# Splits and sums of the output projection's operands, written in another order in a two-layer decoder kernel

## The chip, the cores and the metric

The kernel runs on one core of a Trainium2 chip. The core has five instruction streams that work side by side and meet at semaphores: TensorE (PE, matrix products and transposes; its weight loads are listed as PEld), VectorE (DVE), ScalarE (ACT), GpSimd (POOL) and SyncE (SP), whose stream here only issues transfers between HBM and on-chip memory. The metric is the device time of one execution in microseconds (us), lower is better; the time of a kernel is the median of its runs.

## The reference, cut to what matters

```python
def stick_breaking_attention(q, k, v):           # per 128-query block i
    z = einsum('bqhd,bkhd->bhqk', q_blk, k_blk) * DH ** -0.5
    log_1m = where(mask, log_sigmoid(-z), 0.0)    # mask: key strictly before query
    rev = cumsum(log_1m, axis=3, reverse=True)
    w = where(mask, exp(log_sigmoid(z) + (rev - log_1m)), 0.0)
    out = einsum('bhqk,bkhd->bqhd', w, v_blk)

# layer 1 (layer 0 has gated linear attention in its place)
q = h @ sb_w_q;  o = stick_breaking_attention(q, k_shared, v_shared)
h = layer_norm(DEEPNORM_ALPHA * h + o @ sb_w_o, ln_g[1, 0], ln_b[1, 0])
h = layer_norm(DEEPNORM_ALPHA * h + relu(h @ mlp_w_up[1]) ** 2 @ mlp_w_down[1], ln_g[1, 1], ln_b[1, 1])
```

The sequence has 512 rows, the model 1024 columns, the attention 16 heads of 64, the MLP 4096 columns. All is float32.

## The kernel before, in words

**Arithmetic.** A float32 operand is split into two rounded parts, hi (made by ScalarE, a copy with a narrower type) and lo (the rest, made by VectorE as operand minus hi). A product is then three matmuls: hi by hi, lo by hi, hi by lo (`mm3`, L93 to L95). Splits of weights are `split_tile` (L70 on ScalarE, L72 on VectorE, or on GpSimd where `pool` is handed in); splits of activations are `put` (L98, L99). A weight piece is 128x1024: its raw form arrives by a transfer on SP's queue into one of three buffers (`raw`), its parts go to six buffers each (`hi`, `lo`).

**Stages.** Layer 0 (gated linear attention, LayerNorm, MLP), the shared K and V projection, then layer 1: attention by eight pairs of heads, output projection, LayerNorm, MLP, LayerNorm.

**Attention.** The loop over `p` (L1071) handles one pair in each pass. `weights()` of a pair takes the scores (L943 on PE, into six PSUM banks), adds the mask (L960, VectorE), two sigmoids (L964, L965, ScalarE) and a scan that runs along the keys (L968, VectorE; the listing of instructions calls it SCALAR_TENSOR_TENSOR). `turn()` of the pair in the next pass transposes the five blocks of weights (L977 on PE, four 128x128 transposes each) and moves them out of PSUM into two `wt` tiles, one for each head (L982 on ScalarE). These moves are called evictions below. `outputs()` (L991 on PE) multiplies them with V into one bank, `ops`. Between the transposes PE works on filler: the projection of a later pair's K or Q, for the last pair the first products of the output projection. The query projection's result is split by L931 (ScalarE) and L932 (VectorE).

**Output projection.** It is done with seven products of half size in place of eight, so its operands are sums and differences of the attention output's halves. `o1` holds the output of pairs 0 to 3, `o2` that of pairs 4 to 7; a11 and a21 are the two column halves of `o1`, a12 and a22 those of `o2`. For pairs 4 to 7, `sums` replaces a slice of a21 by a22 minus itself (L1068) and a slice of a11 by its negative plus the difference `less` (both 128x256 on VectorE, L1049 is the second). The names first to seventh stand for the seven operands: `seventh` is the split of `less` (128x1024), `sixth` and `fifth` are the splits of a11 and a21, `third` that of a12 minus a11 (L1049 again, this time 128x1024, `minus(a12, a12, a11)`). Their products are the PE matmuls of L1039. `LATER` (L1147) is the product of a12 or a22 columns themselves (`whole`), whose lo part for the first two slices is made by L1100 of the kernel before. Weights go with them as b1 to b7; b2 comes through `raw` with its lo on GpSimd. `project()` yields after each of four row tiles, and `finish` then does that tile's LayerNorm: `bn_stats` (L177) and `bn_aggr` (L182) on VectorE, reciprocal root on GpSimd (L183, L184), centring on VectorE (L190), eight transposes on PE (L231), scale and shift on ScalarE (L234) and the split of the result (L98, L99), which is the operand of the MLP's first matmuls. The four residual row tiles are `h`; L167 and L169 add product results to them.

**MLP.** `up` (L706) takes its first weights from the list `up0`, four pieces made inside `project()` (L1168, L1172, L1177). Its first half works on row tiles 0 and 1, the second on 2 and 3.

**What sets the order.** A scheduler puts each engine's instructions in an order by readiness and program position; each engine then executes its own list strictly in order and waits where an operand or a buffer is not ready. Instructions wrapped in `keep` (`tc.keep_in_program_order`) hold their written order among themselves. SP's queue of transfers is a list too.

Of the kernel before, what the change touches and what calls it, by code (L numbers as in the profile page):

```python
# [9 lines left out]
F32R = mybir.dt.float32r  # L10
I32 = mybir.dt.int32
AF = mybir.ActivationFunctionType
# [22 lines left out]
def yoco_kernel(ctx: ExitStack, tc: tile.TileContext, x, gla_w_in, gla_w_a2, gla_b_a, gla_norm_g,  # L35
                gla_w_o, kv_w, sb_w_q, sb_w_o, mlp_w_up, mlp_w_down, ln_g, ln_b, out):
    nc = tc.nc
# [20 lines left out]
    def unit(dtype):  # L58
        return big.tile([P, 4, 512], dtype, tag="T", bufs=8, name=nm("T"))
# [19 lines left out]
    def pieces_512(w, r0, nkt, c0, **how):  # L79

        got = []
        for kp in range(nkt // 2):
            hi, lo = split_piece(block(w, r0 + 256 * kp, c0), 2, **how)
            got += [(hi[:, 0, :], lo[:, 0, :]), (hi[:, 1, :], lo[:, 1, :])]
        return got
# [11 lines left out]
    def put(hi, lo, ps, keep=lambda ins: ins, on=None):  # L97
        keep(nc.scalar.activation(hi, ps, AF.Copy))  # L98
        keep((on or nc.vector).tensor_tensor(lo, ps, hi.bitcast(F32), op=ALU.subtract))  # L99
# [909 lines left out]
    def fetch(bs, k, j, onto=False):  # L1009
        for h, b in enumerate(bs):  # L1010
            to = b.rearrange("p (a b) -> p a b", a=2)
            if onto:
                tc.keep_in_program_order(nc.gpsimd.dma_start(out=to, in_=w_o(k, h, j), accum_op=ALU.add))
            else:
                tc.keep_in_program_order(nc.sync.dma_start(out=to, in_=w_o(k, h, j)))
# [48 lines left out]
    ys, us, xs = ([None, None] for _ in range(3))  # L1064
    full = slice(0, 4)

    def sums(k, o):
        tt(a21[:, k, :], o[:, HI], a21[:, k, :], op=ALU.subtract)  # L1068
        minus(a11[:, k, :], o[:, HI], less[:, k, :])

    for p in range(NP):  # L1071
        made = pairs[p].turn()
        take = lambda at: lambda n: [next(made, None) for _ in range(at.get(n, 0))]
        if p + 2 < NP:
            pairs[p + 1].queries()
            if p == 0:
                subtract(keep)
            elif p < NT:
                hs[p].affine(vec, keep)
            pairs[p + 2].keys(take(TAKE))  # L1080
        elif p + 1 < NP:
            pairs[p + 1].queries(take(FILL))
        else:
            mid = take(FILLS)

            def then(n):
                mid(n)
                if n == 11:
                    keep(nc.scalar.activation(o2h[:, 0:2, :], o2[:, 0:2, :], AF.Copy))

            run(STEPS, halves(first), b1, ys, closes=False, mid=mid)
            run(STEPS[:4], halves(seventh), b7, us, closes=False, mid=lambda n: then(8 + n))
        for _ in made:
            pass
        if p < NP - 2:
            pairs[p + 1].weights()
            if p == 1:
                differences(1)()
        if p == NP - 1:
            tt(o2l[:, 0:2, :], o2[:, 0:2, :], o2h[:, 0:2, :].bitcast(F32), op=ALU.subtract)  # L1100
            put(o2h[:, 2, :], o2l[:, 2, :], o2[:, 2, :], keep)
            sums(2, o2[:, 2, :])
            for s in range(2):
                add(s, ys, 0, 0)
        ops = pairs[p].outputs(ALL if p < NP - 2 else LAST)
        if p < 4:
            nc.scalar.activation(o1[:, p, :], ops, AF.Copy)
        else:
            if p == 4:
                o2 = unit(F32)  # L1110
                a12, a22 = o2[:, :, LO], o2[:, :, HI]
            if p == NP - 1:
                put(o2h[:, 3, :], o2l[:, 3, :], ops)
            if p != NP - 2:
                sums(p - 4, ops)
            nc.scalar.activation(o2[:, p - 4, :], ops, AF.Copy)
        if p == 3:
            first = unit(F32R)
            into(first, a11, full)
            less = sbp.tile([P, 4, 256], F32, name="less")  # L1120
            tt(less, a11, a21, op=ALU.subtract)
        if p == NP - 3:
            b1 = pieces_512(sb_w_o[0], 0, 4, 0)
            b22 = wide()
            fetch(b22, 1, 1)
            fetch(b22, 0, 1, True)
        if p == NP - 2:
            b7 = pieces(b22)
            fetch(b22, 0, 0, True)
            b5 = [both(tag).bitcast(F32).rearrange("p a b -> p (a b)") for tag in ("k", "q")]  # L1130
            fetch(b5, 0, 0)
            fetch(b5, 0, 1, True)
            b2 = pieces_512(sb_w_o[0], 512, 4, 0, **pool)
            pairs[p + 1].weights()
            seventh, o2h, o2l = unit(F32R), unit(F32R), unit(F32R)
            into(seventh, less, full)

    b6 = pieces(b22)
    sixth, fifth = unit(F32R), unit(F32R)
    into(sixth, a11, full)  # L1140
    into(fifth, a21, full)
    h3T = Split()
    whole = lambda c0: lambda k, s: tuple(o[:, k, c0 + P * s:c0 + P * s + P] for o in (o2h, o2l))

    def project():
# [6 lines left out]
        run(STEPS, halves(sixth), b6, ys, False, False)  # L1152
        for s in range(2):
            add(s, ys, 1, 0)
        minus(a12, a12, a11)
        third = unit(F32R)
        into(third, a12, full)
        add(0, us, 1, 1)
# [15 lines left out]
        add(0, us, 1, 0, last=True)  # L1174
        yield 2
        yield ~1
        up0.extend(pieces_512(mlp_w_up[1], 512, 4, 0))  # L1177
        run(STEPS[4:], whole(256), b4, us, False)
        add(1, us, 1, 0, last=True)
        yield 3  # L1180
# [79 lines left out]
```

## Time and profile before

| | before |
|---|---|
| median of 3 runs | 1114.59 us (1114.31 to 1114.91) |
| the profiled execution, its own time | 1115.89 us |
| its span, first to last instruction | 1114.2 us |
| mean granted TensorE clock | 0.997 |
| PE busy | 1102.6 us, 99% of the span |
| VectorE busy | 818.2 us, 73% |
| ScalarE busy | 572.1 us, 51% |
| GpSimd busy | 145.4 us, 13% |
| chain that ended last | 90% on PE |

The profiled execution is 1.30 us longer than the median of the runs. In rows of the timeline the first number is the start in us from the span's start, the second the length, then engine, line, operation, output and inputs, shapes, and xN for N instructions merged; in square brackets stands how long the engine had been idle before and what ended it. A matmul's length contains its pipeline, so the next one starts before it has ended. Windows give, for a stretch of time, the busy time of each engine with the count of instructions, then the granted TensorE clock as a share of full speed.

### The profile page before, as it was taken

Reading aid. Unit: us, or ns where it says so; the run is one execution under the profiler, and the core shown is the slowest. Engines: PE = TensorE matmul, PEld = TensorE weight load, DVE = VectorE, ACT = ScalarE, POOL = GpSimd, SP = SyncE. Lnnn points to the kernel's source line nnn. Section 1 sums busy time; section 2 is a strip of 40 time slices with the busy share of each in tenths; the row PEclk is TensorE's granted clock in tenths of the full one; section 3 lists DMA queues with packets and bytes.
Section 4 is the critical chain, followed back from the end, with each engine's and each line's share of the span. In section 5 each row is a group of like instructions: output and inputs, shape, how many; then the busy total and the mean of one; then the engine's idle time right before and its main releaser. Section 6 shows DMA issues by size and latency. Waiting matters only on the chain.

```text
span 1114.2 us, 14380 instructions
## 1 busy us (share of the span) xinstructions
PE 1102.6 (99%) x5503; PEld 913.9 (82%) x5503; DVE 818.2 (73%) x1029; ACT 572.1 (51%) x853; POOL 145.4 (13%) x177
## 2 busy tenths in 40 slices
PE   9999999999999999999999999999999999999997
PEld 7888888898888888888888777788988888888885
DVE  4677639957966856858899886688489767667677
ACT  4455437653533534536675667666545435336363
POOL 1011223200100100122302200211100000001222
PEclk9999999999999999999999999999999999999999
DMA  7441399492670670788746353443937816706774
GB/s 241 130 133 57 115 251 204 138 301 90 188 208 20 201 208 25 196 202 151 225 100 184 107 134 96 101 76 97 302 109 205 237 34 174 223 20 189 177 128 92
DMA packets 111352, 169.06 MB, mean 152 GB/s; under 512 B 13178, under 2 KB 38138, under 8 KB 111284
## 3 DMA queue, kind: packets, MB, share of 16 engines
q1 hardware_dynamic: 86228, 119.39, 32.7%
q0 software_dynamic: 22592, 44.04, 22.8%
q10 hardware_dynamic: 2464, 4.72, 1.2%
q8 instruction: 43, 0.70, 0.3%
q14 instruction: 25, 0.20, 0.1%
HBM read 162.89 MB, written 3.15 MB: 149 GB/s over the span
## 4 chain that ended last, share of the span: by engine, by line
PE 90%; DMA 5%; DVE 2%; issue 1%; POOL 1%; ACT 1%; SPq 0%; POOLq 0%; DVEq 0%; ACTq 0%
PE ps L355 28%; PE ps L93 16%; PE ps L94 16%; PE ps L95 16%; DMA B<-in_gla_w_o_dram 5%; PE ps L796 3%; PE ps L1039 3%; PE ps L991 2%; PE ps L977 2%; PE ps L943 2%; PE ps L231 1%; DVE bst L177 0%; DMA h<-in_x_dram 0%; POOL B L314 0%; PE ps L584 0%
## 5 line engine op out<-in xcount | busy, mean ns | idle before, releaser
L355 PE MATMUL ps<-hi,T 128*128 128x512 f32 x1008 | 313.3, 390 | 0.1
L93 PE MATMUL ps<-T,hi 128*128 128x512 f32 (+1 forms) x776 | 290.2, 375 | 0.0
L94 PE MATMUL ps<-T,hi 128*128 128x512 f32 (+1 forms) x776 | 287.4, 371 | 1.8 <-DVE T L99 1.7
L95 PE MATMUL ps<-T,lo 128*128 128x512 f32 (+1 forms) x776 | 287.0, 370 | 0.0
L72 DVE TENSOR_TENSOR lo<-raw,hi 128x1024 fp32r<-128x1024 f32 x126 | 153.2, 1222 | 95.9 <-ACT hi L70 95.6
L70 ACT ACTIVATE hi<-raw 128x1024 fp32r<-128x1024 f32 x128 | 135.4, 1061 | 169.5 <-PE ps L94 55.1
L355 PEld LDWEIGHTS ps<-hi,T 128*128 128x128 f32 x1008 | 189.0, 188 | 39.8 <-DVE T L99 0.6
L70 ACT ACTIVATE hi<-B 128x1024 fp32r<-128x1024 f32 x118 | 124.4, 1059 | 175.1 <-PE ps L94 105.4
L72 DVE TENSOR_TENSOR lo<-B,hi 128x1024 fp32r<-128x1024 f32 x118 | 143.1, 1223 | 85.8 <-ACT hi L70 85.8
L355 PE MATMUL ps<-lo,T 128*128 128x512 f32 x504 | 196.2, 389 | 0.0
L94 PEld LDWEIGHTS ps<-T,hi 128*128 128x128 f32 x776 | 146.4, 189 | 25.7 <-DVE T L99 2.3
L95 PEld LDWEIGHTS ps<-T,lo 128*128 128x128 f32 x776 | 146.2, 188 | 24.7
L93 PEld LDWEIGHTS ps<-T,hi 128*128 128x128 f32 x776 | 146.1, 189 | 24.3 <-issue 1.0
L314 POOL DMA_DIRECT2D B<-in_mlp_w_down_dram x52 | 62.9, 1262 | 544.2 <-DMA B<-in_mlp_w_down_dram 357.8
L355 PEld LDWEIGHTS ps<-lo,T 128*128 128x128 f32 x504 | 94.7, 188 | 19.6
L169 DVE TENSOR_TENSOR h<-h,ps 128x512 f32<-128x512 f32 x108 | 73.3, 681 | 2.7 <-PE ps L355 2.4
L99 DVE TENSOR_TENSOR T<-s,T 128x1024 fp32r<-128x1024 f32 (+1 forms) x52 | 54.8, 1056 | 9.6 <-ACT T L98 9.6
L98 ACT ACTIVATE T<-s 128x1024 fp32r<-128x1024 f32 (+1 forms) x52 | 48.4, 935 | 21.2 <-DVE s L721 14.1
L968 DVE TENSOR_TENSOR_SCAN c<-r,c 128x384 f32<-128x384 f32 (+2 forms) x64 | 49.4, 819 | 3.3 <-ACT c L965 3.2
L93 PE MATMUL ps<-hi,T 128*128 128x512 f32 x128 | 51.5, 402 | 0.0
L719 ACT ACTIVATE s<-ps 128x512 f32<-128x512 f32 x64 | 38.0, 594 | 25.9 <-PE ps L95 25.2
L95 PE MATMUL ps<-hi,T 128*128 128x512 f32 x128 | 50.3, 393 | 0.0
(212 smaller groups left out, 1295.4 us busy)
## 6 DMA issues: line engine op xcount, KB each, us to landing
raw<-in_mlp_w_up_dram SPq DMA_DIRECT2D x64, 512.0 KB, 5.2
B<-in_mlp_w_down_dram SPq DMA_DIRECT2D x64, 512.0 KB, 5.5
B<-in_mlp_w_down_dram POOLq DMA_DIRECT2D x52, 512.0 KB, 7.4
raw<-in_gla_w_in_dram SPq DMA_DIRECT2D x20, 512.0 KB, 3.8
raw<-in_mlp_w_down_dram SPq DMA_DIRECT2D x16, 512.0 KB, 4.4
B<-in_gla_w_o_dram POOLq DMA_DIRECT2D x14, 512.0 KB, 9.5
raw<-in_kv_w_dram SPq DMA_DIRECT2D x12, 512.0 KB, 4.8
B<-in_gla_w_o_dram SPq DMA_DIRECT2D x8, 512.0 KB, 6.0
```

The lines of the kernel that those rows point to most:

```text
L70: keep(nc.scalar.activation(hi, raw, AF.Copy))
L72: keep((on or nc.vector).tensor_tensor(lo, raw, hi.bitcast(F32), op=ALU.subtract))
L93: keep(nc.tensor.matmul(ps, lhsT=a[0], rhs=b[0], start=first, stop=False))
L94: keep(nc.tensor.matmul(ps, lhsT=a[0], rhs=b[1], start=False, stop=False))
L95: keep(nc.tensor.matmul(ps, lhsT=a[1], rhs=b[0], start=False, stop=last))
L98: keep(nc.scalar.activation(hi, ps, AF.Copy))
L99: keep((on or nc.vector).tensor_tensor(lo, ps, hi.bitcast(F32), op=ALU.subtract))
L169: nc.vector.tensor_tensor(h, h, ps, op=op)
L314: nc.gpsimd.dma_start(out=b.rearrange("p (a b) -> p a b", a=2), in_=weights(k, h, j), accum_op=ALU.add)
L355: nc.tensor.matmul(banks[s], lhsT=a(k, s)[x], rhs=b[k][y], start=opens and (k, x, y) == (0, 0, 0), stop=closes and (k, x, y) == (3, 1, 0), ...
L719: nc.scalar.activation(s2[:, f, :], pss[f], AF.Relu)
L968: nc.vector.tensor_tensor_scan(down, r[:, at][:, ::-1], down, 0.0, op0=ALU.mult, op1=ALU.add)
```

## The change

Five things are written differently.

- `sums` reads the copy in `o2` in place of the PSUM bank, and the copy (L1116 before) is written ahead of it. `sums` takes an optional `keep`.
- The split of `less` into `seventh` moves from the end of pass 6 to behind the evictions of pass 6, pinned with `keep`.
- `sums(2)`, the slice of pair 6, moves from pass 7 to pass 6, behind the scores and weights of pair 7, pinned; b2's pieces are written behind it.
- `minus(a12, a12, a11)` moves from the middle of `project()` to ahead of it, behind the splits of `sixth` and `fifth`, pinned.
- The last two of the four first up-projection pieces are pinned.

```diff
-    def sums(k, o):
-        tt(a21[:, k, :], o[:, HI], a21[:, k, :], op=ALU.subtract)
-        minus(a11[:, k, :], o[:, HI], less[:, k, :])
+    def sums(k, o, keep=lambda ins: ins):
+        keep(tt(a21[:, k, :], o[:, HI], a21[:, k, :], op=ALU.subtract))
+        keep(minus(a11[:, k, :], o[:, HI], less[:, k, :]))
...
         for _ in made:
             pass
+        if p == NP - 2:
+            seventh, o2h, o2l = unit(F32R), unit(F32R), unit(F32R)
+            put(seventh[:, :, LO], seventh[:, :, HI], less, keep)
         if p < NP - 2:
...
             put(o2h[:, 2, :], o2l[:, 2, :], o2[:, 2, :], keep)
-            sums(2, o2[:, 2, :])
             for s in range(2):
...
                 put(o2h[:, 3, :], o2l[:, 3, :], ops)
+            nc.scalar.activation(o2[:, p - 4, :], ops, AF.Copy)
             if p != NP - 2:
-                sums(p - 4, ops)
-            nc.scalar.activation(o2[:, p - 4, :], ops, AF.Copy)
+                sums(p - 4, o2[:, p - 4, :])
...
+            pairs[p + 1].weights()
+            sums(2, o2[:, 2, :], keep)
             b2 = pieces_512(sb_w_o[0], 512, 4, 0, **pool)
-            pairs[p + 1].weights()
-            seventh, o2h, o2l = unit(F32R), unit(F32R), unit(F32R)
-            into(seventh, less, full)
...
     into(sixth, a11, full)
     into(fifth, a21, full)
+    keep(minus(a12, a12, a11))
...
-        minus(a12, a12, a11)
         third = unit(F32R)
...
-        up0.extend(pieces_512(mlp_w_up[1], 512, 4, 0))
+        up0.extend(pieces_512(mlp_w_up[1], 512, 4, 0, keep=keep))
```

How the instructions move is seen at three places. The first is ScalarE in pass 6, from the copy of pair 5's output to the copy of pair 6's; `T<-less` is the hi part of `seventh`, `hi<-raw` the second piece of b2, `q` the hi part of pair 7's query. Before:

```order
L1116 ACTIVATE T_6074<-ps_6247 128x512
L982 ACTIVATE wt_6293<-ps_6295 128x4x128
L98 ACTIVATE T_6456<-less 128x4x256
L982 ACTIVATE wt_6294<-ps_6304 128x4x128
L982 ACTIVATE wt_6293<-ps_6316 128x3x128
L982 ACTIVATE wt_6293<-ps_6316 128x128
L982 ACTIVATE wt_6294<-ps_6326 128x3x128
L982 ACTIVATE wt_6294<-ps_6326 128x128
L70 ACTIVATE hi_6386<-raw_6384 128x1024
L931 ACTIVATE q_6336<-ps_6283 128x512
L982 ACTIVATE wt_6293<-ps_6339 128x2x128
L982 ACTIVATE wt_6294<-ps_6339 128x2x128
```

and after the change:

```order
L1116 ACTIVATE T_6074<-ps_6247 128x512
L982 ACTIVATE wt_6293<-ps_6295 128x4x128
L982 ACTIVATE wt_6294<-ps_6304 128x4x128
L982 ACTIVATE wt_6293<-ps_6316 128x3x128
L982 ACTIVATE wt_6293<-ps_6316 128x128
L982 ACTIVATE wt_6294<-ps_6326 128x3x128
L982 ACTIVATE wt_6294<-ps_6326 128x128
L70 ACTIVATE hi_6459<-raw_6457 128x1024
L931 ACTIVATE q_6336<-ps_6283 128x512
L982 ACTIVATE wt_6293<-ps_6339 128x2x128
L982 ACTIVATE wt_6294<-ps_6339 128x2x128
L98 ACTIVATE T_6346<-less 128x4x256
```

The split of `less` has gone from the second eviction's place to behind the last one. Pair 5's copy stands at the same place in both lists; before it waits for VectorE and PE, now for PE alone.

The second is VectorE at the end of pair 7's scans and in front of the `LATER` product. After the change, from the last scan on:

```order
L968 SCALAR_TENSOR_TENSOR c_6442<-r_6441,c_6442 128x256 x2
L1068 TENSOR_TENSOR T_5008<-T_6074,T_5008 128x256
L1049 SCALAR_TENSOR_TENSOR T_5008<-T_6074,less 128x256
L167 SCALAR_TENSOR_TENSOR h_1637<-h_1637,ps_6463 128x512
L72 TENSOR_TENSOR lo_6565<-d_6271,hi_6563 128x1024
L167 SCALAR_TENSOR_TENSOR h_1638<-h_1638,ps_6476 128x512
L72 TENSOR_TENSOR lo_6569<-d_6272,hi_6567 128x1024
L167 SCALAR_TENSOR_TENSOR h_1639<-h_1639,ps_6503 128x512
L1103 TENSOR_TENSOR T_6348<-T_6074,T_6347 128x1024
```

The second and third rows are `sums(2)`. Before, they stood in front of pair 7's first mask addition (L960), and the row with `h_1637` followed the last scan directly; the last row is `LATER`'s lo part for its first two slices (L1100 before, L1103 after).

The third is VectorE between the centring of row tile 0 and the split of row tile 1 (`h_1637` to `h_1640` are row tiles 0 to 3; `T<-c` the lo parts, in the order tile 0 first half, tile 0 second half, tile 1 first half). Before, from the row behind tile 0's centring:

```order
L167 SCALAR_TENSOR_TENSOR h_1638<-h_1638,ps_6474 128x512
L177 BN_STATS bst_6617<-h_1638 128x6
L182 BN_AGGR mv_6741<-bst_6617 128x2
L169 TENSOR_TENSOR h_1640<-h_1640,ps_6754 128x512
L190 TENSOR_SCALAR h_1638<-h_1638,mv_6741,rs_6743 128x1024
L177 BN_STATS bst_6768<-h_1640 128x6
L72 TENSOR_TENSOR lo_6752<-raw_6748,hi_6750 128x1024
L99 TENSOR_TENSOR T_6578<-c_6770,T_6577 128x4x128
L72 TENSOR_TENSOR lo_6798<-raw_6794,hi_6796 128x1024
L99 TENSOR_TENSOR T_6580<-c_6782,T_6579 128x4x128
L169 TENSOR_TENSOR h_1639<-h_1639,ps_6501 128x512
L72 TENSOR_TENSOR lo_6849<-raw_6845,hi_6847 128x1024
```

there follow a BN_STATS of tile 2 and the split of tile 1's first half. After the change:

```order
L167 SCALAR_TENSOR_TENSOR h_1638<-h_1638,ps_6476 128x512
L169 TENSOR_TENSOR h_1640<-h_1640,ps_6754 128x512
L177 BN_STATS bst_6618<-h_1638 128x6
L177 BN_STATS bst_6768<-h_1640 128x6
L182 BN_AGGR mv_6741<-bst_6618 128x2
L190 TENSOR_SCALAR h_1638<-h_1638,mv_6741,rs_6743 128x1024
L72 TENSOR_TENSOR lo_6752<-raw_6748,hi_6750 128x1024
L99 TENSOR_TENSOR T_6579<-c_6770,T_6578 128x4x128
L72 TENSOR_TENSOR lo_6798<-raw_6794,hi_6796 128x1024
L99 TENSOR_TENSOR T_6581<-c_6782,T_6580 128x4x128
L169 TENSOR_TENSOR h_1639<-h_1639,ps_6503 128x512
L99 TENSOR_TENSOR T_6579<-c_6821,T_6578 128x4x128
```

The lo part of the third MLP piece (`lo_6849`) and tile 2's BN_STATS no longer stand in front of tile 1's split; tile 3's addition and BN_STATS now stand in front of tile 1's BN_AGGR. On ScalarE the hi parts of the third and fourth MLP pieces go behind tile 1's last split in the same way. PE's list moves too, by itself: of the twelve matmuls of the seventh product's second row tile, four stood ahead of the fifth product and eight directly in front of tile 0's transposes (L231); now nine stand ahead of the fifth product and three in front of the transposes. On SP's queue two loads of `mlp_w_down` now stand ahead of the load of the sixth MLP piece, behind which they had stood, the second of them five places further back.

## The prediction, before the run

> **What bounds the kernel now.** I read the page's first part, then PE's waits, then the timeline around each wait.
>
> ```profile
> PE 1102.6 (99%) x5503; PEld 913.9 (82%) x5503; DVE 818.2 (73%) x1029; ACT 572.1 (51%) x853; POOL 145.4 (13%) x177
> ```
> ```profile
> PE ps L991 <- ACT wt L982: 2.0, 1, 2.0
> PE ps L94 <- DVE T L99: 1.7, 1, 1.7
> ```
>
> PE is the bound, so only what makes PE wait or run slowly costs time. Two single waits, of 2.0 and 1.7 us, stand in the region that the change touches; the other three in that view have 1.6 us or less and lie elsewhere or are 0.2. The first wait is the output product of pair 6, the second the first up-projection matmul of the MLP. The first on PE, and under it the same instructions one pair later:
>
> ```profile
> 718.96 0.60 PE L977 MATMUL ps<-ident,c 128*128 128x128 f32 x4
> 721.60 4.61 PE L991 MATMUL ps<-wt,T 128*64 128x256 f32 x28 [2.05 <-ACT wt L982]
> 726.14 2.18 PE L943 MATMUL ps<-k,q 64*128 64x512 f32 x24
> ```
> ```profile
> 738.39 0.60 PE L977 MATMUL ps<-ident,c 128*128 128x128 f32 x4
> 738.92 2.39 PE L991 MATMUL ps<-wt,T 128*64 128x256 f32 x28
> 741.24 0.50 PE L1039 MATMUL ps<-hi,T 128*128 128x512 f32 x1
> ```
>
> Undisturbed, the product starts 0.53 us after its transposes (738.92 - 738.39) and takes 2.32 us (741.24 - 738.92). For pair 6 it should start at 719.49 and end at 721.81; the scores (L943) start at 726.14. So the place costs 4.33 us: 2.11 late, and 2.22 in which the same 28 matmuls take 4.54. ScalarE and VectorE tell why they are late:
>
> ```profile
> 715.91 0.46 ACT L965 ACTIVATE c<-ps 128x256 f32<-128x256 f32 x1
> 718.65 0.60 ACT L1116 ACTIVATE T<-ps 128x512 f32<-128x512 f32 x1 [2.29 <-DVE T L1049]
> 719.62 1.06 ACT L98 ACTIVATE T<-less 128x1024 fp32r<-128x1024 f32 x1
> 720.57 1.70 ACT L982 ACTIVATE wt<-ps 128x512 f32<-128x512 f32 x5
> 722.10 1.11 ACT L70 ACTIVATE hi<-raw 128x1024 fp32r<-128x1024 f32 x1
> 723.52 0.73 ACT L982 ACTIVATE wt<-ps 128x256 f32<-128x256 f32 x2
> ```
> ```profile
> 717.25 0.40 DVE L1068 TENSOR_TENSOR T<-ps,T 128x256 f32<-128x256 f32 x1
> 718.16 0.40 DVE L1049 SCALAR_TENSOR_TENSOR T<-ps,less 128x256 f32<-128x256 f32 x1
> ```
>
> ScalarE's copy of pair 5's output stands idle for 2.29 us until VectorE has read the same bank twice, between its scans; all evictions queue behind the copy, and the split of `less` in the midst of them. The last eviction ends at 724.25 (723.52 + 0.73). Windows show the rest:
>
> ```profile
> 719.10:722.50 3.40, 1.35 (x11) 0.68 (x10) 1.23 (x1) 3.40 (x9) 0.00 (x0) 1.00 0.91 150
> 722.70:725.90 3.20, 3.20 (x23) 2.62 (x20) 0.69 (x1) 1.55 (x4) 2.60 (x2) 0.50 0.00 0
> 773.70:777.10 3.40, 1.70 (x15) 1.66 (x15) 2.95 (x6) 2.21 (x4) 0.79 (x2) 1.00 0.79 242
> ```
>
> After a stretch in which PE was busy for 1.35 of 3.40 us, the granted clock is 0.50 for some 3.2 us. At the second wait PE is busy for 1.70 of 3.40, and the clock stays at 1.00.
>
> I part the 2.22 us. The product has 12 matmuls of 256 columns, then 16 of 128; by 2.32 / (2 x 12 + 16) a narrow one takes 0.058. The last 12 need the evictions that end at 724.25, so at full clock they would end at 724.95. The half clock thus costs 726.14 - 724.95 = 1.19, the late evictions 1.03.
>
> [...]
>
> **The change, part by part.** *Copy first, split of `less` behind the evictions.* The copy now waits for PE alone, so it starts by 716.37 (715.91 + 0.46). From the copy to the b2 split, ScalarE took 722.10 - 718.65 = 3.45, of which the split of `less` was 0.95 (720.57 - 719.62). So 2.50 remain, and the b2 split starts at 718.9; it also waits for a buffer that PE's query projection frees, which ends beside the transposes of 718.96, so 719.2 at the latest. From there to the end of the last eviction it is 724.25 - 722.10 = 2.15: 721.05 to 721.3. The product starts at 719.49 and needs these after 12 wide and 4 narrow matmuls, 1.62 us, at 721.1. It is 0 to 0.2 late, and the scores start at 721.8 to 722.0. The gain is 4.1 to 4.3; I take 4.25.
>
> The split goes on, and its VectorE half is next on the path to pair 7's masks:
>
> ```profile
> 720.71 1.23 DVE L99 TENSOR_TENSOR T<-less,T 128x1024 fp32r<-128x1024 f32 x1 [2.15 <-ACT T L98]
> 726.88 0.43 DVE L1068 TENSOR_TENSOR T<-T,T 128x256 f32<-128x256 f32 x1 [2.46 <-ACT T L1116]
> 727.56 0.49 DVE L960 TENSOR_TENSOR ps<-ps,low 128x128 f32<-128x128 f32 x2
> ```
>
> The hi part ends at about 722.1, the lo part at 723.3, and the first mask follows 1.4 us behind the start of the scores; before it was 727.56 - 726.14 = 1.42, because of `sums(2)`. The one takes the other's place and costs nothing. Were it later still, PE has other products to do until pair 7's last transposes, which stood at 738.39.
>
> *`sums(2)` behind the scans.* It takes 0.68 (727.56 - 726.88), and now stands in front of `LATER`'s lo part:
>
> ```profile
> 735.87 0.66 DVE L167 SCALAR_TENSOR_TENSOR h<-h,ps 128x512 f32<-128x512 f32 x1
> 739.91 1.22 DVE L1100 TENSOR_TENSOR T<-T,T 128x1024 fp32r<-128x1024 f32 x1
> 741.81 0.63 PE L1039 MATMUL ps<-hi,T 128*128 128x512 f32 x2
> ```
>
> VectorE is never idle from 735.87 to there. The lo part ended at 741.13, and `LATER`'s third matmul, the first that reads it, stood at 741.81: 0.68 of slack, just what is now spent. The wait is 0 if all else keeps its distance, 0.8 if VectorE is one instruction of 128x512 or so further behind. I take 0.25, near the lower end, since the other rows of that chain are unchanged.
>
> *`minus(a12, a12, a11)` earlier.* VectorE does it behind the splits of `sixth` and `fifth` as before of them, while PE has `LATER`: 24 matmuls at 0.23. Nothing.
>
> *MLP weights behind the second tile, and PE's filler.* Here is VectorE from tile 0's centring, and PE's answering rows:
>
> ```profile
> 764.20 0.81 DVE L190 TENSOR_SCALAR h<-h,mv,rs 128x1024 f32<-128x1024 f32 x1 [1.02 <-POOL rs L184]
> 764.93 0.68 DVE L167 SCALAR_TENSOR_TENSOR h<-h,ps 128x512 f32<-128x512 f32 x1
> 766.37 0.21 DVE L182 BATCH_NORM_AGGREGATE mv<-bst 128x2 f32<-128x12 f32 x1
> 766.50 0.63 DVE L169 TENSOR_TENSOR h<-h,ps 128x512 f32<-128x512 f32 x1
> 767.59 0.81 DVE L190 TENSOR_SCALAR h<-h,mv,rs 128x1024 f32<-128x1024 f32 x1 [0.45 <-POOL rs L184]
> 768.31 0.69 DVE L177 BATCH_NORM_STATS2 bst<-h 128x6 f32<-128x512 f32 x1
> 772.98 1.22 DVE L72 TENSOR_TENSOR lo<-raw,hi 128x1024 fp32r<-128x1024 f32 x1
> 774.71 0.68 DVE L99 TENSOR_TENSOR T<-c,T 128x512 fp32r<-128x512 f32 x1
> ```
> ```profile
> 765.63 0.39 PE L1039 MATMUL ps<-hi,T 128*128 128x512 f32 x1
> 765.87 1.03 PE L231 MATMUL ps<-ident,h 128*128 128x128 f32 x8
> 769.49 1.03 PE L231 MATMUL ps<-ident,h 128*128 128x128 f32 x8
> 773.11 0.64 PE L93 MATMUL ps<-T,hi 128*128 128x256 f32 x4
> 775.44 0.39 PE L94 MATMUL ps<-T,hi 128*128 128x256 f32 x1 [1.70 <-DVE T L99]
> ```
>
> I keep these times and shift by the rest at the end. Five matmuls move ahead of the fifth product, at 0.23 (765.87 - 765.63 is one) some 1.14. So the third product, and with it tile 0's centring, comes 1.14 later: 765.34 to 766.15, while PE wants tile 0's transposes at 765.87. A wait of 0.3. Behind that, tile 1: its addition at 766.07 (0.73 after the centring's start), then tile 3's addition (0.6) and two BN_STATS (0.6 to 0.7 each) before BN_AGGR at 768.55; 1.22 later, the distance of 766.37 and 767.59, its centring at 769.77, done at 770.58. PE wants its transposes 3.62 (769.49 - 765.87) after the first, at 769.8: a wait of 0.8. Then VectorE has, from the centring to tile 1's split, 774.71 - 767.59 = 7.12, less one L72 (1.13) and two BN_STATS (1.21): 4.78, so the split starts at 774.55, and PE's L94 0.73 behind it (775.44 - 774.71) at 775.28. That is 0.16 earlier than before; the wait there is some 0.45. Three waits with a sum of 1.5 take the place of one of 1.70. As VectorE's chain is unbroken, errors of the first two waits don't add up: the gain is between 0.6 (tile 1's chain 0.45 shorter) and a loss of 0.8 (a BN_STATS more in the way). I take 0.15. The third weight piece's lo part then follows six instructions of 0.6, two BN_AGGR of 0.13, a centring of 0.73 and its own 1.22: done at about 780. PE has the 48 matmuls of the first two pieces, 5.8 us at 0.12, and tile 2's transposes before it, to 781.9.
>
> **Sum:** -4.25 + 0.25 - 0.15 = -4.15; from the profiled execution, 1115.89, that is 1111.74. The median of the runs is 1.30 lower than that execution, close to the 1.19 of the half clock. If the timed runs lack that stretch, their gain is 4.15 - 1.19 = 2.96, and 1114.59 - 2.96 = 1111.6. Both readings meet at 1111.7.
>
> **Rivals.**
> 1. *The timed runs do have the half clock,* and 1.30 is what profiling adds. Then 1114.59 - 4.15 = 1110.4. For it: the three runs lie within 0.6, with no sign of a cost that comes and goes. Against: the 1.30 is explained without it.
> 2. *The evictions stay late,* because the b2 split still stands ahead of the query's and the last two evictions. If its buffer or transfer comes one 128x1024 later, 0.95 are lost: 1112.7.
> 3. *The LayerNorm's waits only move,* with 0.8 lost there and 0.8 at `LATER`: 1111.7 + 0.95 + 0.55 = 1113.2, no difference that can be told.
> [...]
> 5. *Slower.* The load of the sixth MLP piece stands behind two loads of `mlp_w_down`, and its split now in front of tile 3's last one on ScalarE. It gets its buffer when `lo` of the third piece is done, about 779.9 in these times. The second half of `up` reads tile 3's last split at about 794, so the load has until about 792, 12 us, before it decides. Its kind lands in 5.2 us, loads of the other kind in 11.1 here:
>
> ```profile
> raw<-in_mlp_w_up_dram SPq DMA_DIRECT2D x64, 512.0 KB, 5.2
> B<-in_mlp_w_down_dram SPq DMA_DIRECT2D x8, 512.0 KB, 11.1
> ```
> Two of these wholly ahead make 22.2: 10 us lost, 1121.7. Against it: all three may be in flight together.
>
> **How the numbers follow.** Forecast 0.50, rival 1 0.24, rival 2 0.08, rival 3 0.09, rival 4 0.05, rival 5 0.04. The time is the forecast's, 1111.7. The bounds of its terms (4.3 to 4.1 gained; 0 to 0.8 lost; 0.6 gained to 0.8 lost) give 1111.0 to 1113.4 against the profiled execution, both ends unlikely. The range, 1109.9 to 1112.9, leaves out the upper end, rivals 3 to 5 and no more, and takes in rival 1 with 0.5 below it. No change that can be told is within 0.2%, 2.2 us: 1112.4 to 1116.8. The forecast has 0.9 of its chance below that, rival 1 all, rivals 2 and 3 a third: 0.75 faster, 0.04 slower, the rest the same.
>
> **What would show it.** Right: in the changed profile PE's wait at L991 is gone or under 0.3, the scores follow the product's start by 2.3 to 2.5 us, and no window there has a clock of 0.50; ScalarE's copy has no wait for VectorE. L231 shows two waits of about 0.3 and 0.8, L94 one of about 0.5, `LATER` one under 0.3. Wrong: a wait at L991 over 1 us, a sum of the LayerNorm's waits over 2.3, or a wait of the second half of `up` on a split.

## The result, and the profile after

The changed kernel takes 1111.96 us (median of 11 runs, 1111.18 to 1112.70); the kernel before, on the same chip and with eight more runs, 1115.17 us (11 runs, 1114.31 to 1116.73). The ratio is 0.9971, with a 95% interval from 0.9962 to 0.9981: 3.2 us faster. The prediction said 1111.7, in a range from 1109.9 to 1112.9. One further run of the kernel before, made beside e5 to e8, took 1574.49 us at a granted clock of 0.655 and is left out of every comparison below.

The profiled execution of the changed kernel has a span of 1109.5 us against 1114.2. Not all of the 4.7 us is the change. The last transposes of pair 6 stand at 718.30 and stood at 718.96: 0.66 us were gained ahead of every moved instruction. From these transposes to the end it is 391.20 us (1109.5 - 718.30), and was 395.24 (1114.2 - 718.96). So the change gave 4.04 us to this execution; the prediction's sum was 4.15.

PE's waits in the changed kernel's profile (what waits, for whom, us in total, times, longest):

```profile
PE ps L451 <- POOL ident L132: 1.6, 1, 1.6
PE ps L231 <- DVE h L190: 0.8, 3, 0.4
PE ps L94 <- DVE T L99: 0.4, 1, 0.4
PE ps L1039 <- DVE T L1103: 0.2, 1, 0.2
```

The wait of 2.0 us at the output product (L991) is gone. The one of 1.7 at L94 is 0.4. New are two waits for a centring (L231; the third of that row lies in an earlier LayerNorm, and the kernel before has it too) and one at `LATER` (L1039). The timeline of the changed kernel at pair 6, PE first, then ScalarE:

```profile
718.30 0.60 PE L977 MATMUL ps<-ident,c 128*128 128x128 f32 x4
718.83 2.39 PE L991 MATMUL ps<-wt,T 128*64 128x256 f32 x28
721.15 2.19 PE L943 MATMUL ps<-k,q 64*128 64x512 f32 x24
```
```profile
715.53 0.69 ACT L1116 ACTIVATE T<-ps 128x512 f32<-128x512 f32 x1
716.01 2.45 ACT L982 ACTIVATE wt<-ps 128x512 f32<-128x512 f32 x6
718.35 1.06 ACT L70 ACTIVATE hi<-raw 128x1024 fp32r<-128x1024 f32 x1
719.77 0.67 ACT L982 ACTIVATE wt<-ps 128x256 f32<-128x256 f32 x2
720.29 1.09 ACT L98 ACTIVATE T<-less 128x1024 fp32r<-128x1024 f32 x1
```

The product starts 0.53 us after the transposes and takes 2.32, as the undisturbed one of pair 7. The scores (L943) start 2.85 us after the transposes, where it was 7.18. ScalarE's copy no longer waits, the six evictions follow it without a gap, the last two end at 720.44, and the split of `less` comes behind. The clock there (windows about as in the prediction; the granted clock is the number after the five engines):

```profile
719.10:722.50 3.40, 3.40 (x42) 2.74 (x40) 1.78 (x2) 2.77 (x6) 3.01 (x2) 1.00 0.83 142
722.50:725.90 3.40, 3.40 (x25) 2.81 (x23) 2.38 (x6) 2.07 (x4) 0.50 (x1) 1.00 0.80 187
```

PE is busy throughout and the clock full. Further on, PE and VectorE around `LATER` and the LayerNorm, changed kernel:

```profile
733.42 0.60 PE L977 MATMUL ps<-ident,c 128*128 128x128 f32 x4
736.27 0.51 PE L1039 MATMUL ps<-hi,T 128*128 128x512 f32 x1
736.61 0.39 PE L1039 MATMUL ps<-lo,T 128*128 128x512 f32 x1
737.17 0.73 PE L1039 MATMUL ps<-hi,T 128*128 128x512 f32 x2 [0.16 <-DVE T L1103]
737.74 0.39 PE L1039 MATMUL ps<-lo,T 128*128 128x512 f32 x1
761.86 1.06 PE L231 MATMUL ps<-ident,h 128*128 128x128 f32 x8 [0.28 <-DVE h L190]
766.07 1.09 PE L231 MATMUL ps<-ident,h 128*128 128x128 f32 x8 [0.40 <-DVE h L190]
770.75 0.39 PE L94 MATMUL ps<-T,hi 128*128 128x256 f32 x1 [0.36 <-DVE T L99]
```
```profile
762.22 0.68 DVE L169 TENSOR_TENSOR h<-h,ps 128x512 f32<-128x512 f32 x1
762.82 1.28 DVE L177 BATCH_NORM_STATS2 bst<-h 128x6 f32<-128x512 f32 x2
764.02 0.19 DVE L182 BATCH_NORM_AGGREGATE mv<-bst 128x2 f32<-128x12 f32 x1
765.21 0.81 DVE L190 TENSOR_SCALAR h<-h,mv,rs 128x1024 f32<-128x1024 f32 x1 [1.00 <-POOL rs L184]
```

Three waits of 0.28, 0.40 and 0.36 have taken the place of one of 1.70. In the second block tile 3's addition and BN_STATS stand in front of tile 1's BN_AGGR, so that VectorE stands idle for the whole of GpSimd's reciprocal root, 1.00 us, where it had 0.45 left before. From pair 7's last transposes (733.42) to the first L94 it is 37.33 us; before, 37.05 (775.44 - 738.39). So behind pair 6 the change lost 0.28 us net, for all that its waits look smaller.

From L94 to the end it is 338.75 us in both (1109.5 - 770.75; 1114.2 - 775.44 = 338.76): nothing that moved later in the MLP counts.

### The profile page after: what moved, and what is told of

The parts are those of the page before. It is cut to its first block, busy times and chain, and to the rows that moved or that the text cites. A ratio compares the mean times of both kernels' runs of the same rounds, so it can differ in the third digit from the quotient of the medians.

```text
span 1109.5 us, 14388 instructions
## 1 busy us (share of the span) xinstructions
PE 1100.6 (99%) x5503; PEld 912.1 (82%) x5503; DVE 817.8 (74%) x1029; ACT 571.8 (52%) x853; POOL 145.7 (13%) x177
## 4 chain that ended last, share of the span: by engine, by line
PE 94%; DVE 3%; ACT 1%; issue 1%; POOL 0%; POOLq 0%; DVEq 0%; ACTq 0%
PE ps L355 30%; PE ps L93 18%; PE ps L94 18%; PE ps L95 18%; PE ps L796 3%; PE ps L1039 2%; PE ps L977 1%; PE ps L943 1%; PE ps L991 1%; DVE lo L72 1%; PE ps L231 1%; PE ps L584 0%; PE ps L121 0%; DVE h L167 0%; DVE c L968 0%
## 5 line engine op out<-in xcount | busy, mean ns | idle before, releaser
L94 PE MATMUL ps<-T,hi 128*128 128x512 f32 (+1 forms) x776 | 287.5, 371 | 0.5 <-DVE T L99 0.4
L94 PEld LDWEIGHTS ps<-T,hi 128*128 128x128 f32 x776 | 146.4, 189 | 24.2 <-DVE T L99 1.0
```

The lines of the kernel that those rows point to most:

```text
L94: keep(nc.tensor.matmul(ps, lhsT=a[0], rhs=b[1], start=False, stop=False))
```

## The experiments

All are measured in two ways: the time of the runs against the kernel before on the same chip, and in the profile the distance from pair 6's last transposes (L977) to the end of the span, which leaves out what varies ahead of them. That place was at 718.30 to 720.09 us in the twelve profiles, whose programs differ ahead of it by no more than the place of a few VectorE instructions.

| kernel | median, us | ratio to before (95%) | transposes to scores | transposes to end |
|---|---|---|---|---|
| before | 1115.17 | | 7.18 | 395.24 |
| before again (e1) | 1115.26 | 0.9998 (0.9988 to 1.0007) | 5.95 | 394.03 |
| PE kept busy in the wait (e2) | 1114.61 | 0.9991 (0.9981 to 1.0000) | 5.95 | 394.00 |
| copy first alone (e3) | 1112.92 | 0.9977 (0.9967 to 0.9987) | 3.54 | 391.68 |
| split behind the evictions alone (e4) | 1114.07 | 0.9985 (0.9976 to 0.9995) | 5.01 | 393.07 |
| MLP weights' pin alone (e8) | 1114.68 | 0.9996 (0.9986 to 1.0005) | 6.99 | 394.40 |
| the change | 1111.96 | 0.9971 (0.9962 to 0.9981) | 2.85 | 391.20 |
| the change again (e10) | 1111.95 | 0.9966 (0.9954 to 0.9979) | 2.84 | 391.21 |
| the change, minus put back (e5) | 1111.94 | 0.9967 (0.9954 to 0.9980) | 2.85 | 390.73 |
| the change without the MLP pin (e6) | 1113.62 | 0.9987 (0.9978 to 0.9997) | 2.84 | 392.62 |
| e5 with `sums(2)` elsewhere (e7) | 1111.41 | 0.9964 (0.9951 to 0.9978) | 2.85 | 390.19 |
| e7 with tile 1's split first (e9) | 1110.90 | 0.9958 (0.9945 to 0.9971) | 2.85 | 390.02 |

### Is the half clock there in every execution? (e1, no edit)

> The kernel before, unchanged, to see whether its stretch of half clock after the late product of pair 6 is there in each execution. The profiled one has it and a mean granted clock of 0.997; the changed kernel has 0.999 to 1.0. If the half clock belongs to the kernel (rival 1 of the prediction), each timed run shows a mean clock near 0.997 and times lie within 1114.3 to 1116.7 with no second group. [...]

Here is the same place in another execution of the same instructions, PE's timeline and a window:

```profile
718.97 0.60 PE L977 MATMUL ps<-ident,c 128*128 128x128 f32 x4
721.64 3.35 PE L991 MATMUL ps<-wt,T 128*64 128x256 f32 x28 [2.07 <-ACT wt L982]
724.92 2.18 PE L943 MATMUL ps<-k,q 64*128 64x512 f32 x24
```
```profile
722.80:726.20 3.40, 3.40 (x36) 2.63 (x34) 1.24 (x3) 2.08 (x5) 2.86 (x2) 1.00 0.00 0
```

The wait is the same, 2.07 us, and the clock stays full (1.00). The scores start at 724.92, 5.95 us after the transposes; with the half clock it was 7.18. The difference is 1.23, and 1.21 to the end of the span; the prediction's working had 724.95 and 1.19. So the half clock comes and goes. In 72 runs of the kernel before, the mean clock was 0.997 in 27, with a median of 1115.89; it was 1.000 in 16, with a median of 1114.67. The difference of the two groups is 1.22. Between them lie 20 runs at 0.998 and 9 at 0.999, 1115.22 and 1115.08: the times do not fall into two clean groups, since the start of the program varies by as much. Rival 1 does not hold; and the profiled execution of e1, at 1114.71, was below the median of its runs, so profiling adds nothing that can be seen.

The mean clock is a coarse mark too. In the profiles of the kernel before and of the changed one the clock falls to 0.50 once more, at 1111.65 and at 1107.90 (windows of 0.05 us), 3.2 and 4.2 us after PE's last matmul has ended, where it makes no matmul late. In the kernel before the 2.55 us from there to the end of the span take 0.0011 off the mean, the half clock at pair 6 0.0015. e1's profile has a mean of 0.998 without any half clock at pair 6; e8's profile (below) has 0.998 with it. But no profile whose clock is 1.00 at pair 6 has a mean under 0.998 (the changed kernel, e1 to e4, e9), and the runs of the kernels in which the wait at pair 6 is gone, filled or cut to 1.12 us (the change, e2 to e7, e9, e10), also 72, have 0.998 or more. By these figures, an estimate, the 27 runs of the kernel before at 0.997 paid at pair 6, and of the 20 at 0.998 some may have.

In the profile of the kernel before, in windows of 0.05 us, the clock falls at 722.53 and returns at 725.94, 3.41 later. In e8 it is 1.00 from 722.60 to 722.90 and 0.51 from 722.90 to 726.00. The waits ahead are 2.05 and 2.06 us, and 2.07 in e1, where no half clock follows: the length of the wait does not part the executions, and what does is not shown. After the wait of 1.70 us at L94 in the kernel before the clock stays at 1.00 (773.70 to 777.10); in e3, where that wait is 1.72, the matmuls behind it follow at the same 0.12 us.

### Does the idle PE make the clock halve? (e2)

```diff
+            for _ in range(8 if idle else 0):
+                nc.tensor.matmul(ops, lhsT=idle[0], rhs=idle[1], start=True, stop=True, skip_group_check=True)
...
-        ops = pairs[p].outputs(ALL if p < NP - 2 else LAST)
+        ops = pairs[p].outputs(ALL if p < NP - 2 else LAST, (first[:, 0, 0:P], b1[0][0]) if p == NP - 2 else None)
```

> The kernel before with eight added 128x512 matmuls on PE directly ahead of pair 6's output product, into the same bank that the product then overwrites: 8 x 0.23 = 1.8 us of PE work that fill the wait for the evictions and compute nothing that is used. All else keeps its order. Theory (the idle wait made the clock halve, price 1.19 us): no window there with a clock of 0.50, the scores start 6.0 us after the last transposes (7.18 before), the time is 1.2 us below the kernel before. Rival (the slow stretch has another cause, or only the late evictions made the product slow): the scores start 7.2 us after the transposes and the time does not change, or rises.

The added matmuls, then the product and the scores (behind the added lines, this kernel's lines are two further on):

```profile
719.05 2.09 PE L989 MATMUL ps<-hi,T 128*128 128x512 f32 x8
721.37 3.35 PE L993 MATMUL ps<-wt,T 128*64 128x256 f32 x28 [0.23 <-ACT wt L982]
724.65 2.19 PE L943 MATMUL ps<-k,q 64*128 64x512 f32 x24
```

The scores start 5.95 us after the transposes (718.70), to the end it is 394.00: the times of e1's profile without half clock, to 0.03. In the runs it is 0.8 us faster than the kernel before, with an interval that ends at no change. That is less than the 1.2 expected, and as the half clock is paid in some of the runs only (in 27 of 72 it would be about 0.45 us on average), the expectation was too high; the clocks of its ten runs are 0.998 or more. Work that computes nothing thus makes this kernel no slower. The clock is 1.00 from 716.00 to 729.60, with PE busy for 3.17 of the 3.40 us from 719.40, where in e1 it was 1.33. But e1's execution reached the same distances with the wait left in, at a clock of 1.00 too, so this profile alone does not show that the filled wait kept the clock full. The ten clocks agree with it: none is 0.997, where 27 of 72 were in the kernel before.

### Which of the two edits at pair 6 does it? (e3, e4)

e3 has this edit alone:

```diff
-            if p != NP - 2:
-                sums(p - 4, ops)
             nc.scalar.activation(o2[:, p - 4, :], ops, AF.Copy)
+            if p != NP - 2:
+                sums(p - 4, o2[:, p - 4, :])
```

> The kernel before with the copy of each output written ahead of the sums, which then read the copy; nothing else of the change. Theory: the copy no longer waits for VectorE, and the split of `less`, still in the midst of the evictions, costs its 0.95 us there: the product's wait falls to under 1 us, no half clock, the scores start 3.8 us after the last transposes (7.18 before, 2.85 with the whole change), so 3.4 us of the 4.33 are gained; the LayerNorm's wait of 1.70 stays. Rival (the split is what delays the evictions): the gain is 1 us or less.

e4 has this one alone:

```diff
+        if p == NP - 2:
+            seventh, o2h, o2l = unit(F32R), unit(F32R), unit(F32R)
+            put(seventh[:, :, LO], seventh[:, :, HI], less, keep)
...
-            seventh, o2h, o2l = unit(F32R), unit(F32R), unit(F32R)
-            into(seventh, less, full)
```

> The kernel before with only the split of `less` moved behind the evictions of pair 6. Theory: the copy still waits for VectorE's two reads, so the product starts 0.95 us sooner than before, 1.7 after the last transposes; its wait of about 1.1 us no longer halves the clock (1.70 did not, 2.05 did), and the scores start 5.0 after the transposes: a gain of 2.2 us, which with that of the copy alone would come to more than the 4.33 of both. With the half clock still there the scores start 6.2 after and the gain is 1.0. Rival (the copy is all that matters): no gain.

PE's timeline of e3, then of e4:

```profile
719.72 0.60 PE L977 MATMUL ps<-ident,c 128*128 128x128 f32 x4
720.24 3.09 PE L991 MATMUL ps<-wt,T 128*64 128x256 f32 x28
723.26 2.18 PE L943 MATMUL ps<-k,q 64*128 64x512 f32 x24
```
```profile
719.33 0.60 PE L977 MATMUL ps<-ident,c 128*128 128x128 f32 x4
721.05 3.35 PE L991 MATMUL ps<-wt,T 128*64 128x256 f32 x28 [1.12 <-ACT wt L982]
724.34 2.19 PE L943 MATMUL ps<-k,q 64*128 64x512 f32 x24
```

With the copy first, the product starts at once and is stretched from 2.32 to 3.02 us (723.26 - 720.24) by the last two evictions, 0.69 in all. With the split behind, it still waits 1.12 for the copy's sake. Against an execution without half clock (5.95) the copy is worth 2.41 and the split 0.94, both together 3.10. e3 has no wait there and e4 one of 1.12, and no half clock came in either profile (1.00 from 716.00 to 729.60). So the copy is the greater half, the split's 0.95 on ScalarE is the smaller, and 0.25 us of the gain are to be had by either. Both came within 0.3 of what was expected.

### What do the later edits do? (e8, e6, e5)

e8 is the kernel before with the pin of the last two MLP pieces; e6 is the changed kernel without it.

```diff
-        up0.extend(pieces_512(mlp_w_up[1], 512, 4, 0))
+        up0.extend(pieces_512(mlp_w_up[1], 512, 4, 0, keep=keep))
```

> The kernel before with only the pin of the third and fourth MLP weight pieces. Here the pin moves one lo part on VectorE and two hi parts on ScalarE behind tile 1's splits and the wait at the first L94 is the only one there. Theory: L72's 1.13 us leave the chain, the wait of 1.70 falls to about 0.6, the place at pair 6 stays as it is: 1.1 us less than before. Rival: the wait moves to tile 2's transposes or to the third piece's lo part, and nothing is gained.

> The changed kernel without the pin of the third and fourth MLP weight pieces; all else stays. Theory: their hi and lo parts go ahead of tile 1's splits again, so one L72 of 1.13 us comes back into VectorE's chain and the wait at the first L94 grows from 0.36 to 1.5 us, on top of the two waits for centring of 0.7: 1.1 us longer than the changed kernel. Rival (the pin does nothing, the chain ends elsewhere): no difference.

e8, PE's timeline and a window:

```profile
721.65 4.40 PE L991 MATMUL ps<-wt,T 128*64 128x256 f32 x28 [2.06 <-ACT wt L982]
725.99 2.34 PE L943 MATMUL ps<-k,q 64*128 64x512 f32 x24
774.45 0.39 PE L94 MATMUL ps<-T,hi 128*128 128x256 f32 x1 [0.81 <-DVE T L99]
```
```profile
722.80:726.20 3.40, 3.40 (x26) 2.62 (x24) 0.69 (x1) 1.61 (x5) 2.85 (x2) 0.52 0.00 0
```

The wait at L94 falls from 1.70 to 0.81, and the distance to the end from 395.24 to 394.40. The pin is worth 0.84, not the 1.1 expected; in the runs the 0.3 us (1114.98 for the kernel before on the same chip) cannot be told from no change. This profile had the half clock again after an idle wait of 2.06 us, a little later than in the kernel before, so that it reached into the scores (L943, 2.34 us instead of 2.18).

Without the pin, the changed kernel loses 1.42 us to the end, and 1.7 in the median. That is more than expected, and not where it was expected:

```profile
770.95 0.39 PE L94 MATMUL ps<-T,hi 128*128 128x256 f32 x1 [0.36 <-DVE T L99]
782.11 1.09 PE L231 MATMUL ps<-ident,h 128*128 128x128 f32 x8 [1.16 <-DVE h L190]
```

L94 waits no longer than with the pin. PE waits 1.16 us for tile 3's centring, since without the pin the scheduler puts three weight splits, at 774.87, 776.60 and 778.34 on VectorE, around tile 3's addition (776.01) and BN_STATS (777.74), ahead of its centring (781.24). The pin's worth thus depends on what else is in the list: 0.84 in the kernel before, 1.42 in the changed one.

e5 is the changed kernel with the minus back in its old place:

```diff
-    keep(minus(a12, a12, a11))
...
+        minus(a12, a12, a11)
         third = unit(F32R)
```

> The changed kernel with `minus(a12, a12, a11)` put back to the middle of `project()`, not pinned; all else of the change stays. The prediction costed that move at nothing. Theory now: it is this move, not the MLP weights' pin, that sends five matmuls of the filler ahead of the fifth product and tile 3's addition ahead of tile 1's BN_AGGR, since with it back the lists of PE and VectorE are as before at these places. Then the two waits for centring (0.28 and 0.40 us with the change) and the one for tile 1's split (0.36) go, and the span falls by 1.0 us against the changed kernel: a third place of gain, 1.5 to 1.7 us, that the change gave away. Rival: the waits stay, or come back somewhere in the MLP's first half, and the span does not change.

The lists of PE and VectorE do go back: eight filler matmuls in front of tile 0's transposes, tile 3's addition (763.49) behind tile 1's BN_AGGR (763.36). In e5's timeline neither tile 0's transposes nor tile 1's wait. But a wait stays:

```profile
771.42 0.39 PE L94 MATMUL ps<-T,hi 128*128 128x256 f32 x1 [0.83 <-DVE T L99]
```

So the theory was right on what the move of the minus does, and wrong on the sum: 0.47 us are gained (391.20 to 390.73), not 1.0, and the runs cannot tell it from nothing (1111.94 and 1111.96). The 0.83 has its cause in VectorE's list (the same order in e7, quoted below).

### Versions beyond the change (e7, e9), and the change again (e10)

e7 is e5 with `sums(2)` written behind the last pair's split:

```diff
-            sums(2, o2[:, 2, :], keep)
...
                 put(o2h[:, 3, :], o2l[:, 3, :], ops)
+                sums(2, o2[:, 2, :])
```

> The changed kernel with the minus put back as in the run without its move, and `sums(2)` written behind the last pair's split instead of pinned behind the scans; the scheduler then puts its two instructions between pair 7's first masks and first scan, where VectorE stood idle for 1.0 us. Theory: beside the LayerNorm's waits (1.04 us) the wait at `LATER` (0.16) goes too, PE has no wait left between pair 6 and the second half of the MLP, and the span is 1.2 us below the changed kernel's; against the kernel before some 5.5 us in the profile. Rival: pair 7's masks or scans come later by 0.68 and `LATER` or the last transposes wait for that.

The scheduler put the two instructions between pair 7's first masks and first scan, where VectorE was waiting for a sigmoid. The wait at `LATER` is gone, and the distance to the end is 0.54 shorter than e5's and 1.01 shorter than the change's, where 1.2 was expected, with no wait left. What is left is 0.81 at L94, and VectorE's timeline of e7 shows why:

```profile
768.21 0.69 DVE L99 TENSOR_TENSOR T<-c,T 128x512 fp32r<-128x512 f32 x1
768.82 0.68 DVE L169 TENSOR_TENSOR h<-h,ps 128x512 f32<-128x512 f32 x1
769.53 0.69 DVE L177 BATCH_NORM_STATS2 bst<-h 128x6 f32<-128x512 f32 x1
770.14 0.68 DVE L99 TENSOR_TENSOR T<-c,T 128x512 fp32r<-128x512 f32 x1
```

Tile 2's addition and BN_STATS, 1.32 us, stand in front of tile 1's split, which PE is waiting for. e9 pins the split first:

```diff
-                nc.vector.tensor_tensor(h, h, ps, op=op)
+                keep(nc.vector.tensor_tensor(h, h, ps, op=op))
...
-        put(sp.hi[u][:, :, c], sp.lo[u][:, :, c], y)
+        pin = tc.keep_in_program_order if t in getattr(sp, "pin", ()) else (lambda ins: ins)
+        put(sp.hi[u][:, :, c], sp.lo[u][:, :, c], y, pin)
...
     h3T = Split()
+    h3T.pin = (1,)
...
-        add(0, us, 1, 0, last=True)
-        yield 2
         yield ~1
+        add(0, us, 1, 0, last=True, keep=keep)
+        yield 2
```

> The version of the run e7_best, with tile 1's split pinned ahead of tile 2's addition on VectorE (and written so). In e7 the split stood behind that addition and its BN_STATS, which held it for 1.3 us, and PE waited 0.81 at the first L94. Theory: the split then waits only for ScalarE's hi part, the wait at L94 falls to 0.2 or less, and tile 2's centring, now about 2 us later, still comes before its transposes; its third weight piece may make PE wait up to 0.3 once. Span 0.5 to 0.9 us below e7's for the same start, 1.0 to 1.6 below the changed kernel's. Rival: what tile 1 gains is lost whole at tile 2's transposes or at the third piece.

> The changed kernel again beside e9 and the kernel before on one chip, to say what the change is worth with more runs: 3.2 us below the kernel before in the median; mean clocks of 0.999 to 1.0 in all its runs, while the kernel before shows 0.997 in 3 to 5 of 10. If the half clock is the whole of the spread of the kernel before, its runs at 0.999 and 1.0 lie 2.6 to 2.9 us above the changed kernel's, those at 0.997 another 1.2 above.

VectorE's split of tile 1 in e9, and PE behind tile 2's transposes:

```profile
768.38 0.69 DVE L99 TENSOR_TENSOR T<-c,T 128x512 fp32r<-128x512 f32 x1 [0.42 <-ACT T L98]
774.73 1.04 PE L231 MATMUL ps<-ident,h 128*128 128x128 f32 x8
776.49 0.39 PE L95 MATMUL ps<-T,lo 128*128 128x256 f32 x1 [0.48 <-DVE lo L72]
```

The split now waits for ScalarE alone and the wait at L94 is gone. But the third weight piece's lo part is late: on VectorE it stands behind the centrings of tiles 2 and 3, done one right after the other (773.60, 1.70 us for both) after 0.97 us of waiting for GpSimd's reciprocal root. PE waits 0.48 for it: 0.17 us are gained against e7 where 0.5 to 0.9 were expected. The rival was nearly right. e9 is the best of all: 1110.90 in the median and 1.18 us less than the change from the transposes to the end. Beside it on the same chip the change had 1111.95; the intervals of their ratios (0.9945 to 0.9971; 0.9954 to 0.9979) overlap, so the timed runs alone do not part them, the profiles do. The change again showed its waits and distances to within 0.03 us, mean clocks of 0.999 and 1.000 in its five runs, and the kernel before 0.997 in four of eleven. The two of these eleven at 1.000 lie 2.5 and 2.6 us above the change's median, the four at 0.997 another 1.3 in their median, about as expected; one at 0.998 took 1118.94, which nothing here explains.

## Why the prediction was right

**The place at pair 6** was sized at 4.25 us and gave 4.33 (7.18 to 2.85). Its three parts held: in size and in cause the copy's wait and the split's place on ScalarE (e3, e4), and in size the half clock, 1.19 forecast and 1.21 to 1.23 seen (e1). That idling alone brings the half clock was not shown: e1 had the same wait and a clock of 1.00. The last evictions end at 720.44, 2.14 after the transposes, within the 2.1 to 2.3 that the working gave, and the product does not wait for them. The cover of the masks held too: the first mask (L960) is at 722.87, 1.72 behind the scores, where 1.4 was said. The 0.3 more is the split's lo part, which took 1.53 us and not 1.23 (below); nothing waited for it.

**The reading of the median** held in the main. The forecast read the 1.30 us between the profiled execution and the median of three runs as the half clock, took the timed runs to be without it, and put their gain at 2.96. It is 3.21. Without half clock the change is worth 4.04 - 1.21 = 2.83; at least 27 of 72 runs pay 1.2 more, 0.45 on average, which makes 3.28. So the timed runs were not all without it, as the forecast had them; nor do all of them have it, as rival 1 had them (e1). The first three runs, 1114.59 in the median against 1115.17 with eight more, did not show that some pay.

**`LATER`** was sized at 0.25 within 0 to 0.8. The view of waits lists 0.16. The real cost was 0.43 to 0.49: the third matmul is at 737.17 instead of 736.84 (0.33 late), the one behind it comes 0.57 later instead of 0.47; and the stretch from pair 7's transposes to tile 0's is 28.06 us in e5, which has the wait, and 27.57 in e7, which does not. PE's timeline of e5, then of e7:

```profile
734.79 0.60 PE L977 MATMUL ps<-ident,c 128*128 128x128 f32 x4
762.85 1.04 PE L231 MATMUL ps<-ident,h 128*128 128x128 f32 x8
```
```profile
734.73 0.60 PE L977 MATMUL ps<-ident,c 128*128 128x128 f32 x4
762.30 1.03 PE L231 MATMUL ps<-ident,h 128*128 128x128 f32 x8
```

The term was sized at about half of what it measured.

**The minus, "Nothing",** is the one step whose mechanism failed. As an instruction it costs nothing, as forecast. But it is what sent five filler matmuls forward and tile 3's addition ahead of tile 1's BN_AGGR, moves that the prediction put down to the MLP weights and PE's filler and costed there. e5 shows it: with the minus back, both moves are gone, and 0.47 us with them. The sum did not suffer, since the moves themselves were read off the lists and priced; the attribution did.

**The LayerNorm** was to have waits of 0.3, 0.8 and 0.45, and L94 0.16 earlier; listed are 0.28, 0.40 and 0.36. In the distances it is closer: tile 0's transposes came 0.96 later (28.44 against 27.48 from pair 7's transposes; some 0.47 without `LATER`), tile 1's 0.59 (4.21 against 3.62) and L94 regained 1.27 (4.68 against 5.95). Net 0.21 gained without `LATER`, for 0.15 forecast. The chain through VectorE was worked out rightly; the middle wait was 0.2 too long in the forecast.

**The sum** of -4.15 was -4.04 in the profile. That it is so close is in part luck: the 0.2 missed at `LATER` was partly made up by 0.08 more at pair 6 and 0.06 more in the LayerNorm. The rivals 2 to 5 did not come: no late evictions, no half clock at the LayerNorm (1.00 from 758.30 to 778.70, over its three waits; no run shows what would bring one there), no wait in the MLP's second half; rival 3 had 1.5 us more lost behind pair 6 than the forecast's 0.10, and it was 0.18 more. For rival 5, the sixth piece's split did stand in front of tile 3's last one, at 783.81 on ScalarE, and the distance from L94 to the end did not change.

## What to carry to other kernels

A chain that ends in a wait is best sized by the same instructions where they run undisturbed (here one pair later): start after its cause, length, and what follows; the difference splits into late start, late inputs and clock, and each can be checked alone. An instruction moved off the path for nothing can still change where a scheduler puts others: compare all lists with that one move undone before putting a price on the rest. And compare distances between two landmarks instead of adding up listed idle times, and from a landmark behind the start of the program instead of whole spans, when half a microsecond matters.

## What the runs showed of the hardware that was not expected

- The same idle wait of PE, 2.05 to 2.07 us, was followed by half clock in two profiles (before: 0.50 for 3.41 us; e8: 0.52 over a window of 3.40) and by none in a third (e1: 1.00). What parts these executions is not shown. By the mean clock, an estimate (e1, above), it was at least 27 and at most 47 of 72 runs, 38 to 65%. A wait of 1.70 us was followed by a clock of 1.00 (before, at L94).
- A listed wait was less than what it cost: 0.16 listed, 0.43 to 0.49 paid at `LATER`; 0.40 listed, 0.59 paid at tile 1's transposes. At `LATER` the idle time is counted from the listed end of the matmul before, 0.39 us after its start (736.61), where in the kernel before the next one started 0.23 after it (741.58 to 741.81); and the two matmuls behind the wait took 0.57 (737.17 to 737.74) where they took 0.47 before (741.81 to 742.28).
- VectorE's split of `less` took longer in the changed kernel. There its lo part overlaps the end of GpSimd's split of b2:

```profile
719.49 2.37 POOL L72 TENSOR_TENSOR lo<-raw,hi 128x1024 fp32r<-128x1024 f32 x1 [1.76 <-ACT hi L70]
721.42 1.53 DVE L99 TENSOR_TENSOR T<-less,T 128x1024 fp32r<-128x1024 f32 x1 [0.80 <-ACT T L98]
```

It takes 1.53 us instead of the 1.23 of the kernel before. The overlap is 0.44 us (721.86 - 721.42). In e7, which has the split behind the evictions too, the lo part took 1.55; in e1, e2 and e8, which have it in the old place, 1.23. That GpSimd is the cause is not shown.
- Twelve profiles of programs that do nearly the same up to pair 6 reached it at 718.30 to 720.09 us. Part of this is the wait for the first load of h at the program's start (none to 0.5 us in the lists of waits) and a wait for a centring in an earlier LayerNorm, between 500 and 600 us (none in the first two profiles, 0.3 in e10, 0.8 in e3); the rest stays open. The spread is nearly half of what the change gave.
